# A hybrid decoder layer on one Trainium2 core: split input weights stored once and reloaded, and the convolutions given other stretches of the program

## The chip, the cores and the metric

The kernel runs on one core of a Trainium2 chip. The metric is the device time of one execution in microseconds (us). A run of a kernel is one such time; a profile is one further execution, recorded instruction by instruction. The chip's engines go by the profile's names: PE is TensorE (matmuls; PEld its weight loads), DVE is VectorE, ACT is ScalarE, POOL is GpSimd, SP is SyncE, which here only issues transfers (DMAs), in the order of its queue.

## What is computed

One layer of a decoder on 2048 tokens (16 more "meta" tokens are put in front and dropped at the end), with 1024 features, all in float32. Cut to what matters here:

```python
s = layer_norm(concat(meta, x))                       # (2064, 1024)
u = s @ w_in                                          # 1024 -> 2576 columns
c_val, c_gate, q, k, v, r, g_down = split(u)          # 512, 512, 256, 256, 512, 512, 16
h = c_val * sigmoid(c_gate)
conv_out = silu(layer_norm(causal_depthwise_conv(h, width=31) + conv_b))
o = gated_linear_attention(q, k, v, log_sigmoid(g_down @ gate_up + gate_bias) / 16)
gla_out = rms_norm(o) * silu(r)
s = layer_norm(alpha * s + concat(conv_out, gla_out) @ w_out)
s = layer_norm(alpha * s + relu(s @ w_ff1) ** 2 @ w_ff2)
```

## The kernel before, in words

**Number format.** Float32 products are made from two parts. A tile is split into `hi`, the value cast to the rounded type fp32r by ScalarE, and `lo`, the remainder that VectorE subtracts (`split`, L189 to L191). A product is then three matmuls: hi x hi, hi x lo, lo x hi. Weights and activations alike are split on the core, each time that they are loaded.

**Stages.** The 2048 tokens are four groups of 512 (`s` = 0 to 3). For each group the input projection `win_units(s)` runs as a pass over all of `w_in`: in groups 1 to 3 the gate and value columns of the convolution branch (`gate_val`), the attention values V, the forget gate, R, then K and Q; group 0 takes V first, while its tokens are still being normalised, and carries the meta tokens along. A pass needs 40 slabs of weights (256 KB each, 128 partitions x 512 numbers). Then come the output projections of groups 0 and 1 (`wout_units`), feed-forward 1 and 2 of the first half (`ff1s_units`, `ff2_units`, a fast matrix scheme with seven products), the output projections of groups 2 and 3, and the feed-forward of the second half. In feed-forward 1 the first ten weight groups have two of their seven products done ahead, so that five remain (`order`, L1000).

**Slabs.** `load_w` (L193) makes one slab: a raw tile from a pool of four (`rawp`), a DMA on SP's queue (L197 for two row blocks of 256 columns, L200 for one of 512), a slab tile from a ring of ten (`wp`, 512 KB each with both parts) and the split (cast at L190, subtraction at L191). Every pass fetches and splits every slab again: four passes x 40. A channel unit (gate, value, K, Q; `ch_units`, `ch_matmul`, L472 to L474) uses four slabs for 24 matmuls of 512 columns; a token unit (V, R; `tok_units`, L394 to L396) uses one slab for 12.

**Convolution.** Each group's convolution `conv(s)` (L717) takes four channel tiles. It reloads one (`hin`, two buffers, L724), starts the sum on ScalarE (L727) and adds 30 taps with one VectorE instruction each (L730, out `cacc`), so 120 for a group. Then it transposes, normalises (L737 to L758) and stores its half of the mixer's input (`mixd`, L760), which the output projection loads and splits (`mix_load`, tile `mraw`).

**Order.** `Program` holds the matmul work as a list of units with costs, and side streams: generators that are stepped in proportion to the costs that have passed between a start and an end unit (`prog.side`, L1337 and on). The convolutions are side streams, and each of their steps carries a lowered priority (`later`, L764). A scheduler then arranges the instructions of each engine by its own estimate of when they can run; each engine runs them in that order. So a convolution's stretch is a guide, and the built order says where its steps stand. `bounds[s]` is the first unit of pass `s`, `m_wout` that of the output projection, `m_f20` that of feed-forward 2 of the first half, `W[s].gv_end` the end of a pass's gate and value units. `prog.defer(n, fn)` runs `fn` n units later.

**Feed-forward 1.** Each weight group loads two raw tiles (`w1r`, L971, in the ring of ten), forms operand sums from them on VectorE (L978; `s` is the first difference), splits them into operands (`wop`), multiplies (L1007 to L1009), combines the products of the group before on VectorE (L1041; `p`, `u`, `a`, `h`, `s` are its tiles) and stores results through SP's queue (`hor`, L1014). A w1r load stands behind such stores in SP's queue.

Of the kernel before, what the change touches and what calls it, by code (L numbers as in the profile page):

```python
# [10 lines left out]
F32 = mybir.dt.float32  # L11
F32R = mybir.dt.float32r
# [5 lines left out]
P = 128  # L18
# [6 lines left out]
KD = D // P  # L25
# [23 lines left out]
CONV_LATE = 100  # L49
# [96 lines left out]
def hymba_kernel(ctx: ExitStack, tc: tile.TileContext, x, meta, ln_in_g, ln_in_b, w_in, small, gate_up,  # L146
                 w_out, ln1_g, ln1_b, w1, w2, ln2_g, ln2_b, out):
    nc = tc.nc
# [4 lines left out]
    wp = ctx.enter_context(tc.tile_pool(name="wp", bufs=RING))  # L153
# [4 lines left out]
    dp = ctx.enter_context(tc.tile_pool(name="dp", bufs=1, space=bass.MemoryType.DRAM))  # L158
# [19 lines left out]
    prog = Program(RING)  # L178

    def mm_tile():  # L180
        return mmp.tile([P, 512], F32, tag="mm", name="mm")
# [7 lines left out]
    def split(hi, lo, src, eng=None):  # L189
        nc.scalar.copy(hi, src)  # L190
        (eng or nc.vector).tensor_tensor(out=lo, in0=src, in1=hi.bitcast(F32), op=ALU.subtract)  # L191

    def load_w(src, nk, eng=None):  # L193
        def fn():
            raw = rawp.tile([P, 512], F32, tag="raw", name="raw")
            if nk == 2:
                nc.sync.dma_start(out=raw.rearrange("p (k c) -> p k c", k=2),  # L197
                                  in_=src.rearrange("(k p) c -> p k c", p=P))
            else:
                nc.sync.dma_start(out=raw, in_=src)  # L200
            sl = wp.tile([P, 2, 512], F32R, tag="w", name="wsl")
            split(sl[:, 0, :], sl[:, 1, :], raw, eng)
            return sl
        return prog.load(fn)

    def loads_ch(w, c0):
        return [load_w(w[k2 * 256:(k2 + 1) * 256, c0:c0 + 256], 2) for k2 in range(KD // 2)]

    def loads_tok(w, c0):
        return [load_w(w[k * P:(k + 1) * P, c0:c0 + 512], 1) for k in range(KD)]  # L210

    def rstd_of(out_, var, n):
        p = out_.shape[0]
# [81 lines left out]
    def load_x(s, tt):  # L295
        t = xin[s, tt] = pa.tile([P, D], F32, tag="xin", name="xin", bufs=2)
        nc.sync.dma_start(out=t, in_=x[s * SUB + tt * P:s * SUB + (tt + 1) * P, :])

    def prep_tile(s, tt):
        if s or tt == 0:  # L300
            load_x(s, tt)
        t = xin[s, tt]
        if s == 0 and tt == 0:
            nc.sync.dma_start(out=A.g, in_=ln_in_g.partition_broadcast(P))
            nc.sync.dma_start(out=A.b, in_=ln_in_b.partition_broadcast(P))
            load_x(0, 1)
        yield
        st = stats_bn(t) if s == 0 and tt < NBN else stats_act(t, None, pa, "sg")
        if s == 0 and tt == 0:
            prog.pre(RING)  # L310
            consts()
        yield
        yield from ln_apply(t, st, A.g, A.b)
        nc.sync.dma_start(out=s0d[s][tt], in_=t)
        yield from transpose_split(t, xt[s], tt)
# [129 lines left out]
    W = {}  # L445

    def win_units(s):
        w = W[s] = NS()
# [41 lines left out]

        def first_units(c0, evac):
            nonlocal xtm
            ls = [load_w(w_in[k * P:(k + 1) * P, c0:c0 + 512], 1, nc.gpsimd if k % 2 else None) for k in range(KD)]

            def unit(tt):
                for _ in prep_tile(0, tt):
                    pass
                if 0 < tt + 1 < TT - 1:
                    load_x(0, tt + 2)
                ps = mm_tile()  # L500
                for k in range(KD):
                    tok_mm(ps, prog.slot[ls[k]], k, tt)
                evac(tt, ps)

            def unit_meta():
                nonlocal xtm
                xtm = prep_meta()
                um = meta_matmul(lambda k: [prog.slot[ls[k]][:, hl, :] for hl in range(2)], 512)
                pv = gl_tile()
                nc.tensor.matmul(pv, i2, um, start=True, stop=True)  # L510
                w.vm = pa.tile([P, 512], F32, tag="og", name="vm")
                nc.scalar.copy(w.vm, pv)

            for tt in range(TT):
                prog.add(lambda tt=tt: unit(tt), ls, 5.2)
            prog.add(unit_meta, ls, 3.5)
# [246 lines left out]
    CONV_N = CT * CW + TT * 3  # L763

    def later(gen, offset):
        while True:
            with tc.high_priority(offset=-offset):
                try:
                    next(gen)
                except StopIteration:  # L770
                    return
            yield
# [534 lines left out]
    m_wout = prog.mark()  # L1307
# [8 lines left out]
    m_f20 = ff_units(0, late[0])  # L1316
    m_w2 = prog.mark()
# [15 lines left out]
    bounds = m_win + [m_wout]  # L1333
# [2 lines left out]
    for s in range(NSUB - 1):  # L1336
        prog.side(gla(s), GLA_N, bounds[s + 1], W[s + 1].gd)  # L1337
    prog.side(gla(NSUB - 1), GLA_N, m_wout - 1, m_wout)
    prog.side(later(conv(0), CONV_LATE), CONV_N, W[0].gv_end, bounds[1] + 16)
    prog.side(later(conv(1), CONV_LATE), CONV_N, W[1].gv_end, bounds[3])  # L1340
    prog.side(later(conv(2), 100), CONV_N, W[3].gv_end, m_f20)
    prog.side(later(conv(3), 100), CONV_N, m_f20, m_w2 - 4)
    prog.side(ln2_sub(0), 3 * TT, m_w2, m_w3)
    prog.side(ln2_sub(1), 3 * TT, m_w3, m_ff1)
    prog.emit()
# [30 lines left out]
```

## Time and profile before

| what | us |
|---|---|
| median of the runs shown (2109.33, 2111.32, 3585.48) | 2111.32 |
| the profiled execution's own time | 2108.08 |
| its span, first to last instruction | 2106.4 |
| TensorE busy in it | 2021.8 |
| VectorE busy | 1650.7 |
| ScalarE busy | 1005.3 |

A matmul is counted as busy until its modelled end, though the next one starts before, so the busy time of TensorE tells only where it stood quite still. Read beside it the count of matmuls in a stretch. Lines are those of the kernel before; a line can be a helper's (L190 and L191 are all splits), so the tile's name says which use it is. "<-" behind a wait names what ended it.

### The profile page before, as it was taken

The page shows a single profiled execution, that of the slowest core. Times are in us where ns is not written, and L with a number is a line of the kernel's source. Part 1 is how long each engine was busy: PE and PEld are TensorE (multiplying, and loading weights), DVE is VectorE, ACT ScalarE, POOL GpSimd, SP SyncE. Part 2 cuts the span into 40 slices and gives each one's busy share as a digit, 9 for nine tenths or more (in the row PEclk, how much of TensorE's full clock was granted, in tenths as well). Part 3 has the DMA queues.
Part 4 walks back from the last instruction along what each step waited for, and adds up shares of the span by engine and source line. Part 5 has one row for each costly group of instructions (what it writes and reads, how often), then busy time and mean ns, then how long its engine had stood idle before and what let it go on. Part 6 is the DMA issues. An engine that isn't in the chain of part 4 may idle for free. (4 is left out here: it accounts for less than half of the span.)

```text
span 2106.4 us, 26294 instructions
## 1 busy us (share of the span) xinstructions
PE 2021.8 (96%) x9144; PEld 1647.0 (78%) x9144; DVE 1650.7 (78%) x2658; ACT 1005.3 (48%) x1720; POOL 93.7 (4%) x104
## 2 busy tenths in 40 slices
PE   6999999999989999999999999999999999999996
PEld 4878878878777777778778788777777787788885
DVE  6599989989988677776699999579877765644875
ACT  3564474554543454455653434455644554433342
POOL 3000100100000000000000000011000000000001
PEclk9999999999999999999999999999999999999998
DMA  5533434534346556654899877277666548965761
GB/s 185 172 111 107 147 110 122 162 90 130 107 125 205 191 185 209 205 180 144 284 331 390 311 251 273 70 242 252 198 204 206 183 140 291 320 203 197 251 221 70
DMA packets 245285, 409.39 MB, mean 194 GB/s; under 512 B 21424, under 2 KB 115856, under 8 KB 245152
## 3 DMA queue, kind: packets, MB, share of 16 engines
q1 hardware_dynamic: 226144, 368.91, 53.2%
q10 hardware_dynamic: 19008, 38.81, 4.9%
q8 instruction: 72, 1.18, 0.2%
q14 instruction: 61, 0.50, 0.1%
HBM read 297.29 MB, written 110.35 MB: 194 GB/s over the span
## 5 line engine op out<-in xcount | busy, mean ns | idle before, releaser
L730 DVE SCALAR_TENSOR_TENSOR cacc<-hin,sm,cacc 128x512 f32<-128x512 f32 x480 | 344.6, 745 | 2.0
L1218 PE MATMUL mm<-op 128*128 128x512 f32 x544 | 213.3, 392 | 7.0 <-ACT op L190 7.0
L190 ACT CAST wsl<-raw 128x512 fp32r<-128x512 f32 x224 | 136.6, 620 | 168.0 <-PE mm L396 40.5
L1219 PE MATMUL mm<-op 128*128 128x512 f32 x544 | 212.8, 391 | 0.0
L1220 PE MATMUL mm<-op 128*128 128x512 f32 x544 | 211.3, 390 | 0.0
L190 ACT CAST op<-wr 128x1024 fp32r<-128x1024 f32 x92 | 92.5, 1051 | 223.0 <-PE mm L1220 163.2
L191 DVE TENSOR_TENSOR op<-wr,op 128x1024 fp32r<-128x1024 f32 x92 | 108.9, 1219 | 80.2 <-ACT op L190 80.1
L191 DVE TENSOR_TENSOR wsl<-raw,wsl 128x512 fp32r<-128x512 f32 x220 | 149.4, 690 | 24.9 <-ACT wsl L190 24.6
L1007 PE MATMUL gl<-x,wop 128*128 128x512 f32 x384 | 152.1, 397 | 7.8 <-DVE a L1041 3.0
L394 PE MATMUL mm<-xt,wsl 128*128 128x512 f32 x384 | 153.8, 400 | 0.0
L395 PE MATMUL mm<-xt,wsl 128*128 128x512 f32 x384 | 152.4, 397 | 0.0
L396 PE MATMUL mm<-xt,wsl 128*128 128x512 f32 x384 | 152.2, 397 | 0.0
L1008 PE MATMUL gl<-x,wop 128*128 128x512 f32 x384 | 150.7, 392 | 0.0
L1009 PE MATMUL gl<-x,wop 128*128 128x512 f32 x384 | 150.2, 392 | 0.0
L1218 PEld LDWEIGHTS mm<-op 128*128 128x128 f32 x544 | 102.7, 189 | 29.6 <-ACT op L190 7.9
L190 ACT CAST wop<-w1r 128x512 fp32r<-128x512 f32 x152 | 91.0, 616 | 67.0 <-DVE w1r L978 38.0
L1219 PEld LDWEIGHTS mm<-op 128*128 128x128 f32 x544 | 102.7, 189 | 21.3
L1220 PEld LDWEIGHTS mm<-op 128*128 128x128 f32 x544 | 102.4, 188 | 21.4 <-DVE op L191 0.2
L191 DVE TENSOR_TENSOR op<-lr,op 128x1024 fp32r<-128x1024 f32 (+1 forms) x92 | 104.8, 1172 | 16.7 <-ACT op L190 16.7
L191 DVE TENSOR_TENSOR wop<-w1r,wop 128x512 fp32r<-128x512 f32 x152 | 103.7, 687 | 17.5 <-ACT wop L190 16.8
L1007 PE MATMUL mm<-xt,wop 128*128 128x512 f32 x256 | 100.9, 397 | 5.2 <-ACT a L1047 5.2
L1007 PE MATMUL mm<-x,wop 128*128 128x512 f32 x256 | 100.4, 396 | 1.5 <-ACT x L190 0.8
(282 smaller groups left out, 4811.5 us busy)
## 6 DMA issues: line engine op xcount, KB each, us to landing
wr<-in_w_dram SPq DMA_DIRECT2D x120, 512.0 KB, 6.1
lr<-hor SPq DMA_DIRECT2D x108, 512.0 KB, 6.0
raw<-in_w_in_dram SPq DMA_DIRECT2D x160, 256.0 KB, 2.9
w1r<-in_w_dram SPq DMA_DIRECT2D x64, 512.0 KB, 5.2
wr<-td SPq DMA_DIRECT2D x40, 512.0 KB, 5.4
raw<-in_w_out_dram SPq DMA_DIRECT2D x64, 256.0 KB, 4.1
hor<-s SPq DMA_DIRECT2D x64, 256.0 KB, 3.0
raw<-in_w_dram SPq DMA_DIRECT2D x40, 256.0 KB, 4.0
```

The costliest lines, as they stand in the source:

```text
L190: nc.scalar.copy(hi, src)
L191: (eng or nc.vector).tensor_tensor(out=lo, in0=src, in1=hi.bitcast(F32), op=ALU.subtract)
L394: nc.tensor.matmul(ps, wh, mov(k, 0), start=(k == 0), stop=False)
L395: nc.tensor.matmul(ps, wh, mov(k, 1), start=False, stop=False)
L396: nc.tensor.matmul(ps, wl, mov(k, 0), start=False, stop=(k == KD - 1))
L730: nc.vector.scalar_tensor_tensor(out=acc, in0=h[:, j:j + SUB], scalar=wc(j), in1=acc, op0=ALU.mult, op1=ALU.add)
L1007: nc.tensor.matmul(ps, wh, X[i][:, k, 0, :], start=start and k == 0, stop=False, skip_group_check=not start)
L1008: nc.tensor.matmul(ps, wh, X[i][:, k, 1, :], start=False, stop=False, skip_group_check=not start)
L1009: nc.tensor.matmul(ps, wl, X[i][:, k, 0, :], start=False, stop=(k == 3), skip_group_check=not start)
L1218: nc.tensor.matmul(ps, lh, rt[n][:, p, 0, :], start=(q == 0 and p == 0), stop=False)
L1219: nc.tensor.matmul(ps, lh, rt[n][:, p, 1, :], start=False, stop=False)
L1220: nc.tensor.matmul(ps, ll, rt[n][:, p, 0, :], start=False, **ends)
```

## The change

In the first group's pass each split slab is also stored to a DRAM tile (`wkd`, 512 KB, one unit after its load). In the other three passes the slab is loaded from there with one DMA straight into the ring, without a raw tile and without a split. Apart from that, the four convolutions have other start and end units.

```diff
--- before.py
+++ after.py
@@ -190,8 +190,14 @@
         nc.scalar.copy(hi, src)
         (eng or nc.vector).tensor_tensor(out=lo, in0=src, in1=hi.bitcast(F32), op=ALU.subtract)
 
-    def load_w(src, nk, eng=None):
+    wkd = {}
+
+    def load_w(src, nk, eng=None, kept=None):
         def fn():
+            if kept is not None and kept in wkd:
+                sl = wp.tile([P, 2, 512], F32R, tag="w", name="wsl")
+                nc.sync.dma_start(out=sl.bitcast(F32), in_=wkd[kept].bitcast(F32))
+                return sl
             raw = rawp.tile([P, 512], F32, tag="raw", name="raw")
             if nk == 2:
                 nc.sync.dma_start(out=raw.rearrange("p (k c) -> p k c", k=2),
@@ -200,14 +206,18 @@
                 nc.sync.dma_start(out=raw, in_=src)
             sl = wp.tile([P, 2, 512], F32R, tag="w", name="wsl")
             split(sl[:, 0, :], sl[:, 1, :], raw, eng)
+            if kept is not None:
+                d = wkd[kept] = dp.tile([P, 2, 512], F32R, name=f"wkd{kept}")
+                prog.defer(1, lambda: nc.sync.dma_start(out=d.bitcast(F32), in_=sl.bitcast(F32)))
             return sl
         return prog.load(fn)
 
     def loads_ch(w, c0):
-        return [load_w(w[k2 * 256:(k2 + 1) * 256, c0:c0 + 256], 2) for k2 in range(KD // 2)]
+        return [load_w(w[k2 * 256:(k2 + 1) * 256, c0:c0 + 256], 2, kept=c0 + k2 if w is w_in else None)
+                for k2 in range(KD // 2)]
 
     def loads_tok(w, c0):
-        return [load_w(w[k * P:(k + 1) * P, c0:c0 + 512], 1) for k in range(KD)]
+        return [load_w(w[k * P:(k + 1) * P, c0:c0 + 512], 1, kept=c0 + k if w is w_in else None) for k in range(KD)]
 
     def rstd_of(out_, var, n):
         p = out_.shape[0]
@@ -490,7 +500,8 @@
 
         def first_units(c0, evac):
             nonlocal xtm
-            ls = [load_w(w_in[k * P:(k + 1) * P, c0:c0 + 512], 1, nc.gpsimd if k % 2 else None) for k in range(KD)]
+            ls = [load_w(w_in[k * P:(k + 1) * P, c0:c0 + 512], 1, nc.gpsimd if k % 2 else None, kept=c0 + k)
+                  for k in range(KD)]
 
             def unit(tt):
                 for _ in prep_tile(0, tt):
@@ -1336,10 +1347,10 @@
     for s in range(NSUB - 1):
         prog.side(gla(s), GLA_N, bounds[s + 1], W[s + 1].gd)
     prog.side(gla(NSUB - 1), GLA_N, m_wout - 1, m_wout)
-    prog.side(later(conv(0), CONV_LATE), CONV_N, W[0].gv_end, bounds[1] + 16)
-    prog.side(later(conv(1), CONV_LATE), CONV_N, W[1].gv_end, bounds[3])
-    prog.side(later(conv(2), 100), CONV_N, W[3].gv_end, m_f20)
-    prog.side(later(conv(3), 100), CONV_N, m_f20, m_w2 - 4)
+    prog.side(later(conv(0), CONV_LATE), CONV_N, W[0].gv_end, bounds[1] + 14)
+    prog.side(later(conv(1), CONV_LATE), CONV_N, bounds[1] + 14, bounds[2] + 21)
+    prog.side(later(conv(2), CONV_LATE), CONV_N, bounds[2] + 21, m_wout)
+    prog.side(later(conv(3), CONV_LATE), CONV_N, m_wout, m_f20 + 60)
     prog.side(ln2_sub(0), 3 * TT, m_w2, m_w3)
     prog.side(ln2_sub(1), 3 * TT, m_w3, m_ff1)
     prog.emit()
```

**In the built order, VectorE in feed-forward 1, first half, one of the groups with five products.** `s`, `p`, `u`, `a`, `h` are as above; lines of the changed kernel stand 11 higher there (L989 is L978, L1052 is L1041, L741 is L730). Before:

```order
L978 TENSOR_TENSOR s_7506<-w1r 128x512
L1041 TENSOR_TENSOR p_7479<-p_7479,gl 128x512
L1041 TENSOR_TENSOR p_7479<-p_7479,a_7334 128x512
L978 TENSOR_TENSOR w1r<-w1r 128x4x128 x2
L1041 TENSOR_TENSOR u_7458<-u_7458,mm 128x512
L978 TENSOR_TENSOR w1r<-w1r 128x4x128
L191 TENSOR_TENSOR wop<-w1r,wop 128x4x128 x2
L1041 TENSOR_TENSOR s_7528<-h_7336,u_7458 128x512
```

and now:

```order
L989 TENSOR_TENSOR s_7456<-w1r 128x512
L741 SCALAR_TENSOR_TENSOR cacc<-hin,sm,cacc 128x512 x2
L1052 TENSOR_TENSOR p_7429<-p_7429,gl 128x512
L741 SCALAR_TENSOR_TENSOR cacc<-hin,sm,cacc 128x512
L1052 TENSOR_TENSOR p_7429<-p_7429,a_7285 128x512
L989 TENSOR_TENSOR w1r<-w1r 128x4x128
L1052 TENSOR_TENSOR u_7409<-u_7409,mm 128x512
L989 TENSOR_TENSOR w1r<-w1r 128x4x128
L741 SCALAR_TENSOR_TENSOR cacc<-hin,sm,cacc 128x512
L989 TENSOR_TENSOR w1r<-w1r 128x4x128
L191 TENSOR_TENSOR wop<-w1r,wop 128x4x128
```

Four steps of the last convolution (L741) stand between the difference and the first operand split; a fifth stands ahead of the difference.

**SP's queue in the first pass, from the value product of the first channel tile.** `hd` is the store of the convolution's input, `s0d` that of the normalised tokens, `raw` a load of weights. Before:

```order
L297 DMA xin<-in_x_dram 128x1024 x2
L197 DMA raw<-in_w_in_dram 128x2x256 x8
L314 DMA s0d_0_96<-xin 128x1024
L609 DMA hd_0_108<-h 128x512
L613 DMA hd_0_112<-h 128x30
L297 DMA xin<-in_x_dram 128x1024
L197 DMA raw<-in_w_in_dram 128x2x256 x2
```

and now, where `wkd` is the store of a split slab:

```order
L211 DMA wkd_682<-wsl 128x1024
L211 DMA wkd_688<-wsl 128x1024
L620 DMA hd_0_108<-h 128x512
L624 DMA hd_0_112<-h 128x30
L324 DMA s0d_0_96<-xin 128x1024
L203 DMA raw<-in_w_in_dram 128x2x256 x4
L307 DMA xin<-in_x_dram 128x1024
L211 DMA wkd_837<-wsl 128x1024
L211 DMA wkd_843<-wsl 128x1024
```

Stores of slabs now stand ahead of the stores of `hd`, and the next raw loads behind both.

**SP's queue in the second pass, at its first value products.** Before:

```order
L724 DMA hin<-hd_2_110 128x542
L197 DMA raw<-in_w_in_dram 128x2x256 x8
L724 DMA hin<-hd_3_111 128x542
L609 DMA hd_0_112<-h 128x512
L613 DMA hd_0_116<-h 128x30
L197 DMA raw<-in_w_in_dram 128x2x256 x2
L200 DMA raw<-in_w_in_dram 128x512
L711 DMA mixd_1_233<-go 512x1x128
```

and now (L199 loads a split slab, L735 the convolution's input):

```order
L199 DMA wsl<-wkd_682 128x1024
L199 DMA wsl<-wkd_688 128x1024
L735 DMA hin<-hd_2_110 128x542
L620 DMA hd_0_112<-h 128x512
L624 DMA hd_0_116<-h 128x30
L199 DMA wsl<-wkd_837 128x1024
L199 DMA wsl<-wkd_843 128x1024
L199 DMA wsl<-wkd_849 128x1024
L199 DMA wsl<-wkd_855 128x1024
```

The slab loads stand in the queue where raw loads stood, one for one, with the convolution's loads among them.

## Rows read from the trace of the kernel before

**Rows 1.** The page, busy time of one engine (share of the span) and instructions.

```profile
PE 2021.8 (96%) x9144; PEld 1647.0 (78%) x9144; DVE 1650.7 (78%) x2658; ACT 1005.3 (48%) x1720; POOL 93.7 (4%) x104
```

**Rows 2.** Windows: stretch; length; busy PE, PEld, DVE, ACT, POOL (instructions); clock; DMA share; GB/s.

```profile
0.00:75.00 75.00, 57.09 (x246) 44.20 (x247) 45.00 (x83) 32.96 (x58) 17.23 (x26) 0.98 0.57 184
...
595.00:695.00 100.00, 96.25 (x473) 78.23 (x472) 84.29 (x169) 40.01 (x92) 8.60 (x8) 1.00 0.53 175
...
750.00:901.00 151.00, 146.46 (x633) 115.77 (x632) 118.48 (x189) 74.80 (x134) 0.00 (x0) 1.00 0.61 199
...
1055.00:1170.00 115.00, 113.92 (x503) 94.37 (x504) 108.03 (x116) 49.27 (x57) 0.00 (x0) 1.00 0.97 365
...
1800.00:1850.00 50.00, 50.00 (x222) 41.40 (x221) 28.28 (x25) 19.82 (x22) 0.00 (x0) 1.00 0.90 314
```

**Rows 3.** Waits of TensorE, 150 to 300 and 450 to 600 us: total, times, longest.

```profile
PE tp L751 <- ACT cn L748: 2.0, 2, 1.2
...
PE tp L578 <- DVE e L572: 3.7, 1, 3.7
...
PE tp L751 <- ACT cn L748: 2.3, 3, 1.1
...
PE mm L410 <- ACT gd L403: 1.9, 1, 1.9
```

**Rows 4.** Windows, the stretch behind the longest of those waits.

```profile
583.40:590.20 6.80, 6.01 (x16) 4.88 (x17) 6.01 (x11) 3.29 (x7) 0.00 (x0) 0.50 0.49 155
```

**Rows 5.** The page, costliest groups: busy, mean ns; idle before.

```profile
L190 ACT CAST wsl<-raw 128x512 fp32r<-128x512 f32 x224 | 136.6, 620 | 168.0 <-PE mm L396 40.5
...
L191 DVE TENSOR_TENSOR wsl<-raw,wsl 128x512 fp32r<-128x512 f32 x220 | 149.4, 690 | 24.9 <-ACT wsl L190 24.6
```

**Rows 6.** Groups by line, VectorE's convolution steps, 0 to 600 and 1050 to 1345 us.

```profile
L730 DVE SCALAR_TENSOR_TENSOR cacc<-hin,sm,cacc 128x512 f32<-128x512 f32 x329 | 236.2, 744 | 0.8
...
L730 DVE SCALAR_TENSOR_TENSOR cacc<-hin,sm,cacc 128x512 f32<-128x512 f32 x120 | 85.5, 746 | 0.8
```

**Rows 7.** Timeline of VectorE and SP in feed-forward 1: start, us, instruction, wait before it.

```profile
800.21 0.69 DVE L978 TENSOR_TENSOR s<-w1r 128x512 f32<-128x512 f32 x1 [2.55 <-DMA w1r<-in_w_dram]
...
808.01 0.68 DVE L1041 TENSOR_TENSOR u<-u,p 128x512 f32<-128x512 f32 x1
...
808.72 0.32 SPq L1014 DMA_DIRECT2D hor<-u  x1
...
809.15 0.38 SPq L971 DMA_DIRECT2D w1r<-in_w_dram  x1
...
815.13 0.69 DVE L978 TENSOR_TENSOR s<-w1r 128x512 f32<-128x512 f32 x1 [2.82 <-DMA w1r<-in_w_dram]
...
815.74 0.68 DVE L1041 TENSOR_TENSOR p<-p,gl 128x512 f32<-128x512 f32 x1
```

**Rows 8.** Waits of VectorE, 750 to 901 us.

```profile
DVE s L978 <- DMA w1r<-in_w_dram: 18.6, 10, 2.8
...
DVE w1r L978 <- DMA w1r<-in_w_dram: 8.9, 9, 2.6
```

**Rows 9.** The page, DMA issues: KB each, median us to landing.

```profile
wr<-in_w_dram SPq DMA_DIRECT2D x120, 512.0 KB, 6.1
...
raw<-in_w_in_dram SPq DMA_DIRECT2D x160, 256.0 KB, 2.9
...
xin<-in_x_dram SPq DMA_DIRECT2D x16, 512.0 KB, 3.7
```

**Rows 10.** Waits of TensorE, 1050 to 1350 and 1350 to 1450 us.

```profile
PE mm L1218 <- ACT ac L1233: 2.0, 1, 2.0
...
PE mm L1218 <- ACT op L190: 1.9, 1, 1.9
...
PE tp L751 <- ACT cn L748: 1.3, 2, 0.7
```

**Rows 11.** Waits of SP's queue, 150 to 600 us.

```profile
SPq L724 <- DVE cacc L730: 37.3, 8, 10.9
```

## The prediction, on record before the changed kernel ran

> **What bounds the kernel now.** I read the page's busy times first, then the windows stage by stage, then the waits of each engine inside a stage, and last the timeline of the stage where a chain of waits shows. TensorE is busy for 2021.8 of 2106.4 us [rows 1], so the whole kernel is nearly a stream of matmuls, and only its gaps can be won or lost. How full a stage is I take from matmul counts. In an untroubled window of 50 us there are 222 matmuls of 512 columns [rows 2], that is 0.2252 us each. The first half's stage "feed-forward 1" (FF1), 750 to 901 us, shows 633 matmuls in 151 us: 633 x 0.2252 = 142.6 us at most, as a few of them are shorter, so over 8 us of it are gaps, though its busy column leaves 4.5 [rows 2].
>
> The Trainium skill ("Trainium Kernel Development and Optimization", Performance Expectations) says that matmul busy time is a bad measure of distance to the limit because matmuls are pipelined, and that weight-load busy time is a good one. The trace agrees: weight loads are 41.40 of 50 us in the full window and 115.77 of 151 us here, so 151 x (1 - 0.767 / 0.828) = 11 us of gaps. By the busy column TensorE would be within 3% of its limit here and the loop described below would hardly bind; by the page it binds already, and what lengthens it is paid in full.
>
> In the four input-projection passes (0 to 600 us) the waits that TensorE names after 150 us are short: on the transposes of the convolution's norm, once on the key transposes (3.7 us) and once on the gate (1.9) [rows 3]. None of these waits names a weight slab, although every slab is cast on ScalarE and subtracted on VectorE before use. After the 3.7 us gap the granted clock is 0.50, its lower level, for 6.8 us [rows 4]: 16 matmuls in 6.8 us instead of about 30. So 3.2 us more belong to that gap.
>
> **The change, part by part.**
>
> *Splits removed.* Three passes x 40 slabs = 120 slabs need neither the cast (620 ns) nor the subtraction (690 ns) [rows 5]: 120 x 0.620 = 74 us of ScalarE and 120 x 0.690 = 83 us of VectorE. Neither engine ends the chain in these passes; TensorE waits on them only in the rows named. The waits after 150 us are 2.0 + 3.7 + 2.3 + 1.9 [rows 3] and three smaller ones of 2.2 together, 12.1 us, and 3.2 us of clock: at most 15 us to win, at least nothing. I take 8: the key gap and its clock loss (6.9), since the slab splits and the splits of the mixer's input that stand between its instructions on VectorE and ScalarE leave or move ahead, and 1 of the rest. What is late next there is the gate chain, which in the last pass now has 12 convolution steps queued ahead of its subtraction.
>
> *Convolution moved.* Each convolution is 120 steps of 745 ns on VectorE. The order of VectorE shows where they stand. Before, 321 of 480 stand ahead of the last pass's final key product; the trace has 329 by 600 us, and all 120 of the last convolution in feed-forward 2 (FF2) [rows 6]; FF1 has none. Now 360 stand ahead of that key product (39 more, 29 us, against 83 removed), 56 between there and the first main load of FF1 (39 before), and 64 in FF1's main groups, where none stood. FF2 loses all of its 120, 89 us.
>
> *FF1, the term that decides.* Its first ten groups of five products run in a loop over VectorE, the SP queue and a transfer. The rows show one turn: a sum `u` at 808.01, its store and the w1r load behind it in SP's queue at 808.72 and 809.15, the operand difference waiting 2.82 us for that load and starting at 815.13; the same instruction of the turn before started at 800.21 [rows 7]. So a turn is 14.9 us, while 60 matmuls need 60 x 0.2252 = 13.5. Over 750 to 901 us VectorE waits 18.6 us on the first w1r and 8.9 on the second [rows 8]: about 2.8 + 0.7 a turn. Into each turn the new order puts five convolution steps: one ahead of the difference (inside the 2.8 us wait: free), two right behind it and one between the two `p` sums, and one between the w1r sums. An instruction of 0.69 us is followed after 0.61 (815.13 to 815.74) [rows 7], so a step of 0.745 takes some 0.66 of the engine. The three in the middle add 2.0 us ahead of a w1r sum that waited 0.7, so 1.3 remain; the one between the sums adds 0.66. Both lie on the way from the landing of w1r to the `u` store that lets the next w1r go: 14.9 + 1.96 = 16.8 us a turn. Groups 2 to 9 carry this pattern: 8 x 1.96 = 15.7 us. Groups 0 and 1 also carry the norm of the second half and I leave them at nothing; from group 10 a turn has seven products, 84 x 0.2252 = 18.9 us of TensorE, which covers 16.8. Bounds: 0, if the 27.5 us of waits took all steps; 51 steps x 0.745 = 38 if none were hidden. A gain is excluded, as work is only added there. I take 15.
>
> The Trainium skill ("Perfetto Trace Analysis", Tensor Engine Instruction) notes that the queues of VectorE and ScalarE are strictly first in, first out. The trace agrees: the `p` sum behind the waiting difference starts only at 815.74 [rows 7]. If the queue could be passed, the term would be 0; this is the first rival's time.
>
> *Output projection, 595 to 695 us.* 56 - 39 = 17 more steps, 12.7 us, on a VectorE that was busy for 84.29 of 100 [rows 2]. Between 0 and 12.7; I take 3, since 15.7 us were idle but not where the steps stand.
>
> *Loads of split slabs.* 120 loads of 512 KB instead of 256 KB. The old ones landed in 2.9 us; a 512 KB load of 4 KB rows, as x's, in 3.7, the slowest kind in 6.1 [rows 9]. They go straight into the ring of ten slabs, so SP waits for a slab to come free, and the four raw buffers that ran ahead are gone. A gate or value unit is 24 matmuls, 5.4 us. Its slab is freed some 4 us before the second unit of its kind ends, then a value unit and half a gate unit pass before the slot's new slab is used: 4.1 + 5.4 + 2.7 = 12.2 us against 3.7 to 6.1. I take 0; 6 us are spare.
>
> *Stores in the first pass.* 40 stores of 512 KB, 21 MB, and each waits in SP's queue for its subtraction, with the raw loads of the next slabs behind it. In 0 to 75 us the core moved 184 GB/s [rows 2], 13.8 MB; with 22 stores 25.3 MB, or 338 GB/s, below the 365 that it sustains at 1055 to 1170 us [rows 2]. A group of raw loads now leaves after the splits of the group before: it loses its head start, at worst load, cast and subtraction, 2.9 + 0.62 + 0.69 = 4.2 us a group. The ring holds ten slabs, so most is hidden. Bounds 0 and 8 groups x 4.2 = 34; I take 2, near the hidden end, since ten slabs in hand last longer than 4.2 us.
>
> *FF2 and the second output projection.* FF2 at 1055 to 1170 us holds 503 matmuls, 113 us of 115 [rows 2]: nearly full with the convolution in it. Its waits are 2.0 and 1.9 us on ScalarE, and 1.3 us on the convolution's norm behind it [rows 10]. Gain 0 to 5; I take 3.
>
> **Sum.** The profiled execution took 2108.08 us. 2108.1 + 15 + 3 + 0 + 2 - 8 - 3 = 2117. The two closely agreeing runs are 2109.33 and 2111.32, some 2 above it: 2119 us, 0.4% over the median shown. A measurement of this kernel can tell about 2% (42 us) from no change, so this is "the same".
>
> **Rivals.**
> *The steps fit into the waits.* If the w1r landing moves with the new order, or takes less than the 6 us of rows 7, FF1 costs nothing: 2119 - 15 = 2104. For it: 27.5 us of waits stand against 51 x 0.66 = 34 us of steps, nearly enough. Against it: one step in five stands in the long wait. 0.25.
> *The first pass starves.* Raw loads behind stores behind splits: if the four gate and value groups each lose 4.2 us, 17 in place of 2: 2134. For it: 338 of 365 GB/s is near what the core sustains. Against it: the ring. 0.10.
> *The three later passes starve (the slower side).* SP's queue has waited up to 10.9 us at one load of the convolution's input for VectorE [rows 11]. A slab load behind that leaves 10.9 us late; with 6.1 to land, 17.0 against 12.2, TensorE loses 4.8 us. It decides from a block over 6.1 us at the moment a gate or value slab comes free; at 4 groups in 3 passes 12 x 4.8 = 58: 2177. Against it: only four of these loads fall in a pass, mostly in the token units, where a slab has ten units of 2.7 us. 0.05.
> *It doesn't do what it says.* If VectorE stays the late engine in the passes, the 8 us are not won: 2127; inside the range, and I give it no chance of its own.
> The forecast itself has 0.60, with 2108 to 2130 as its own range.
>
> **Numbers.** The range 2094 to 2140 reaches the first rival with some more of the 15 us of the passes won (2104 - 10), and the second with 6 over; it leaves out the third and the ends. Slower by over 2% (above 2153.5): 0.05 of the third rival and 0.01 of several terms at their ends, 0.06. Faster by over 2% (below 2069): all gains at their bounds give 2108 - 15 - 5 = 2088, so 0.02 for what I don't see. Within 2%: 0.92.
>
> **What would show it.** In the changed profile: no cast or subtraction of input slabs after the first pass; conv steps of 745 ns between w1r sums in FF1, with the difference instructions 16 to 17 us apart where they were 14.9, and fewer matmuls per us there; the 3.7 us key gap and its half-clock stretch gone; FF2 no longer than before by its matmul count. The forecast is wrong if the turn stays near 15 us, if TensorE's waits in 150 to 600 us name wsl, or if the first 150 us grow by over 10.

## The result, and the profile after

The changed kernel takes 2143.74 us (median of five runs, 2142.65 to 2147.34) against 2109.33: the ratio is 1.0175, 95% interval 1.0163 to 1.0187. One of the five runs of the kernel before took 3585.48 us, and the ratio leaves it out, so it is not quite the quotient of the two medians. That is 34 us slower, within the 2% called "the same", but outside the predicted range (2094 to 2140).

The page after, busy times, answers to [rows 1]; its DMA issues, KB each and median us to landing, to [rows 9]:

```profile
span 2141.9 us, 25907 instructions
...
PE 2035.9 (95%) x9144; PEld 1657.1 (77%) x9144; DVE 1580.3 (74%) x2538; ACT 943.1 (44%) x1608; POOL 92.8 (4%) x104
...
wsl<-wkd SPq DMA_DIRECT2D x120, 512.0 KB, 4.7
...
wkd<-wsl SPq DMA_DIRECT2D x40, 512.0 KB, 4.7
```

VectorE lost 120 instructions and 70 us of work, ScalarE 112 and 62 us; the span grew by 35.5. So less work on these two engines did not make the kernel faster.

Where the time went is read from matmuls that both kernels have. The view of one line's instructions gives their first and last start (the two times after "ns"). Before, L394 is a product of the channel units, with which a pass ends, L867 of the output projections (first and second half), L1218 of FF2. (The kernel's description has two ranges of lines the wrong way round: `ch_matmul` is L394 to L396, the token units are L472 to L474.)

```profile
L394 PE MATMUL mm<-xt,wsl x384: 387/389/628, 46.1 to 598.6; 128*128 128x512 f32 x192
...
L867 PE MATMUL mm<-wsl,xt x64: 387/389/585, 600.4 to 711.5; 128*128 128x512 f32 x64
...
L1218 PE MATMUL mm<-op x272: 389/389/499, 1041.3 to 1341.2; 128*128 128x512 f32 x136
L1218 PE MATMUL mm<-op,ox x96: 387/389/497, 1067.1 to 1355.3; 128*128 128x512 f32 x96
...
L867 PE MATMUL mm<-wsl,xt x64: 387/389/476, 1359.2 to 1454.5; 128*128 128x512 f32 x64
...
L1218 PE MATMUL mm<-op,ox x96: 389/389/389, 1807.5 to 2089.7; 128*128 128x512 f32 x96
```

and after (L404, L878, L1229):

```profile
L404 PE MATMUL mm<-xt,wsl x384: 387/389/628, 49.8 to 611.4; 128*128 128x512 f32 x192
...
L878 PE MATMUL mm<-wsl,xt x64: 387/389/482, 613.7 to 730.7; 128*128 128x512 f32 x64
...
L1229 PE MATMUL mm<-op x272: 387/389/792, 1067.1 to 1382.2; 128*128 128x512 f32 x136
L1229 PE MATMUL mm<-op,ox x96: 387/389/478, 1098.3 to 1393.1; 128*128 128x512 f32 x96
...
L878 PE MATMUL mm<-wsl,xt x64: 389/389/400, 1395.1 to 1487.6; 128*128 128x512 f32 x64
...
L1229 PE MATMUL mm<-op,ox x96: 388/389/390, 1843.0 to 2125.2; 128*128 128x512 f32 x96
```

The differences of these ends, stage by stage and from the unrounded times: four passes +12.7 us, output projection +6.5, FF1 up to FF2's first matmul +6.5, FF2 +12.0, second output projection -4.6, the rest +2.4; together 35.5, the whole growth of the span. The same table for the other kernels stands below.

**FF1.** The window that answers to [rows 2] (the same stretch, 19 us later), and one turn, which answers to [rows 7]:

```profile
769.00:920.00 151.00, 140.53 (x589) 109.47 (x588) 134.66 (x218) 67.25 (x123) 0.00 (x0) 0.98 0.57 186
```

```profile
839.79 0.69 DVE L989 TENSOR_TENSOR s<-w1r 128x512 f32<-128x512 f32 x1 [1.56 <-DMA w1r<-in_w_dram]
840.39 1.41 DVE L741 SCALAR_TENSOR_TENSOR cacc<-hin,sm,cacc 128x512 f32<-128x512 f32 x2
841.72 0.68 DVE L1052 TENSOR_TENSOR p<-p,gl 128x512 f32<-128x512 f32 x1
842.32 0.75 DVE L741 SCALAR_TENSOR_TENSOR cacc<-hin,sm,cacc 128x512 f32<-128x512 f32 x1
...
849.05 0.69 DVE L1052 TENSOR_TENSOR u<-u,p 128x512 f32<-128x512 f32 x1
849.77 0.32 SPq L1025 DMA_DIRECT2D hor<-u  x1
...
855.66 0.69 DVE L989 TENSOR_TENSOR s<-w1r 128x512 f32<-128x512 f32 x1 [1.65 <-DMA w1r<-in_w_dram]
```

There are 589 matmuls where there were 633, 44 x 0.2252 = 9.9 us fewer. The turn from difference to difference is 15.9 us (14.9 before). Over the eight turns from the third difference to the eleventh, the timeline gives 128.3 us, 115.9 before, so 16.0 and 14.5 a turn. The steps stand where the order had them: from difference to `u` sum it now takes 849.05 - 839.79 = 9.26 us (808.01 - 800.21 = 7.80 in [rows 7]), and the wait for w1r is shorter (1.6 us, 2.8 before).

**FF2.** TensorE's waits there (1060 to 1260 us; total, times, longest), and VectorE around the longer of the norm's:

```profile
PE tp L762 <- ACT cn L759: 7.0, 3, 4.2
PE mm L1229 <- ACT op L190: 6.6, 1, 6.6
```

```profile
1171.46 1.23 DVE L1179 TENSOR_TENSOR wr<-wr 128x1024 f32<-128x1024 f32 x1 [6.00 <-DMA wr<-td]
1172.60 0.69 DVE L770 TENSOR_TENSOR cy<-cy,csg 128x512 f32<-128x512 f32 x1
1173.20 0.69 DVE L750 BATCH_NORM_STATS2 cbn<-tp 128x6 f32<-128x512 f32 x1
```

The last convolution's norm now stands in the middle of FF2. Its statistics are queued on VectorE behind an operand sum that waits 6.00 us for a transfer; its transposes (L762) stand in TensorE's own queue, in front of matmuls that are ready.

**Passes.** TensorE's waits, 180 to 612 us, after; they answer to [rows 3]:

```profile
PE tp L762 <- ACT cn L759: 4.9, 4, 2.6
PE mm L420 <- ACT gd L413: 4.1, 1, 4.1
PE tp L719 <- DVE og L714: 3.4, 7, 0.8
PE tp L748 <- DVE cacc L741: 2.2, 2, 1.1
```

The 3.7 us key gap is gone, and none names wsl. The gate waits 4.1 us instead of 1.9, and the transposes of convolution and attention wait more often. The first pass ends 7.0 us later than before (181.1 us, 174.1 before); the second is 6.2 us longer, the third 10.0 longer, the last 10.4 shorter.

That the gap is gone does not show that the change removed it. The run e10 below leaves the passes as they were: up to 600 us its trace has the same instructions of TensorE, VectorE and ScalarE as that of before, in the same order. There the key gap is 0.9 us, in this line of TensorE's waits from 540 to 700 us:

```profile
PE tp L578 <- DVE e L572: 0.9, 1, 0.9
```

No half-clock stretch stands behind it, and the passes end 4.8 us earlier than in the profile of before. In e11 the gap is 2.1 us and they end 3.3 us earlier. So most of the 3.7 us belonged to that one execution.

**The clock.** Windows of five of the half-clock stretches after (the column before the DMA share is the granted clock), beside [rows 4]:

```profile
301.60:305.00 3.40, 2.78 (x11) 2.59 (x12) 2.98 (x7) 3.02 (x7) 0.99 (x1) 0.50 0.57 185
567.90:571.30 3.40, 3.39 (x8) 2.74 (x9) 3.22 (x6) 2.54 (x5) 0.00 (x0) 0.50 0.00 0
...
864.80:868.20 3.40, 3.40 (x10) 2.62 (x9) 3.40 (x6) 2.15 (x5) 0.00 (x0) 0.50 0.65 222
1083.30:1090.10 6.80, 5.16 (x12) 4.10 (x13) 5.89 (x9) 6.26 (x7) 0.55 (x1) 0.50 0.77 257
1178.80:1182.20 3.40, 3.26 (x10) 2.78 (x11) 2.63 (x3) 2.16 (x6) 0.00 (x0) 0.51 1.03 380
```

Between start-up and the final tail the trace has 54.4 us of such stretches, 20.4 before. At half rate the 34 more cost some 17 us, an estimate (a little less where TensorE also stood still): nearly half of the loss. The mean granted clock, too, is lower in all five runs of the changed kernel (0.983 to 0.985; 0.993 in the profile of before). They come behind the waits named above: the one at 301.6 behind a wait on the norm (the 2.6 us one), the one at 567.9 behind the gate's, the one at 864.8 behind a wait of 1.7 us in FF1, the one at 1083.3 behind the 6.6 us wait, the one at 1178.8 behind the norm's.

### The profile page after: what moved, and what is told of

Read it like the earlier page. It is cut to its first block, busy times and chain, and to the rows that moved or that the text cites. A ratio compares the mean times of both kernels' runs of the same rounds, so it can differ in the third digit from the quotient of the medians.

```text
span 2141.9 us, 25907 instructions
## 1 busy us (share of the span) xinstructions
PE 2035.9 (95%) x9144; PEld 1657.1 (77%) x9144; DVE 1580.3 (74%) x2538; ACT 943.1 (44%) x1608; POOL 92.8 (4%) x104
## 5 line engine op out<-in xcount | busy, mean ns | idle before, releaser
L741 DVE SCALAR_TENSOR_TENSOR cacc<-hin,sm,cacc 128x512 f32<-128x512 f32 x480 | 344.7, 747 | 4.9 <-ACT cacc L738 1.8
L1229 PE MATMUL mm<-op 128*128 128x512 f32 x544 | 214.9, 395 | 12.9 <-ACT op L190 12.9
L404 PE MATMUL mm<-xt,wsl 128*128 128x512 f32 x384 | 153.1, 399 | 0.0
L1229 PEld LDWEIGHTS mm<-op 128*128 128x128 f32 x544 | 103.7, 191 | 35.2 <-ACT op L190 13.7
L1018 PE MATMUL mm<-x,wop 128*128 128x512 f32 x256 | 103.3, 406 | 9.8 <-ACT wop L190 6.7
L190 ACT CAST op<-lr 128x1024 fp32r<-128x1024 f32 (+1 forms) x92 | 89.6, 1010 | 37.1 <-DMA lr<-hor 37.1
L1019 PE MATMUL mm<-x,wop 128*128 128x512 f32 x256 | 103.0, 402 | 0.1
```

What stands on the lines that cost most here:

```text
L404: nc.tensor.matmul(ps, wh, mov(k, 0), start=(k == 0), stop=False)
L741: nc.vector.scalar_tensor_tensor(out=acc, in0=h[:, j:j + SUB], scalar=wc(j), in1=acc, op0=ALU.mult, op1=ALU.add)
L1018: nc.tensor.matmul(ps, wh, X[i][:, k, 0, :], start=start and k == 0, stop=False, skip_group_check=not start)
L1019: nc.tensor.matmul(ps, wh, X[i][:, k, 1, :], start=False, stop=False, skip_group_check=not start)
L1229: nc.tensor.matmul(ps, lh, rt[n][:, p, 0, :], start=(q == 0 and p == 0), stop=False)
```

## The experiments

The starting theory: the loss comes from where the convolutions stand. The rival: it comes from the 160 transfers of 512 KB and their places in SP's queue. Each stage's growth in us against the profile of before, from the view shown above; "us" are medians of runs, each ratio against the kernel before on the same chip. A profile is one execution, so single entries under some 5 us say little: the passes differ by 4.8 us between before and e10, with the same instructions there in the same order, and the first pass by 4.4 between e1 and e6, with the same instructions too. The profiled run of e1 took 4.3 us less than the median of its runs, those of e4 and e6 took 5.1 and 4.4 more.

| run | us | ratio, 95% | passes | out 1 | FF1 | FF2 | out 2 | rest |
|---|---|---|---|---|---|---|---|---|
| changed kernel | 2143.7 | 1.0175 | +12.7 | +6.5 | +6.5 | +12.0 | -4.6 | +2.4 |
| e1 reload alone | 2112.9 | 1.0008-1.0036 | +1.3 | -0.3 | -2.7 | +0.6 | +1.0 | +0.5 |
| e2 spread alone | 2138.4 | 1.0124-1.0163 | +10.7 | +10.9 | +4.5 | +10.6 | -5.4 | -1.2 |
| e3 conv 3 lines back | 2139.9 | 1.0137-1.0168 | +9.3 | +6.6 | +9.0 | +3.5 | +0.7 | +2.3 |
| e4 stores on ScalarE | 2141.6 | 1.0134-1.0168 | +11.4 | +6.4 | +6.4 | +12.4 | -1.1 | +3.0 |
| e5 conv 2, 3 back | 2123.7 | 1.0041-1.0079 | +13.6 | +0.1 | -0.7 | -1.4 | +0.7 | +0.6 |
| e6 conv 0, 1 back | 2133.5 | 1.0064-1.0125 | +3.4 | +6.7 | +12.3 | +10.7 | -6.4 | +2.7 |
| e7 store in pass 2 | 2109.4 | 0.9982-1.0012 | +1.1 | 0.0 | -0.3 | -1.4 | +0.3 | +1.0 |
| e8 store in pass 3 | 2110.7 | 0.9976-1.0009 | -0.6 | -0.3 | -0.5 | +3.8 | +0.4 | +2.0 |
| e9 mixer loads later | 2109.4 | 0.9989-1.0011 | -4.8 | +2.8 | -0.2 | -0.5 | +2.0 | +0.3 |
| e10 steps behind | 2133.2 | 1.0098-1.0136 | -4.8 | +0.3 | +14.2 | +12.5 | -0.2 | +0.8 |
| e11 steps ahead | 2123.2 | 1.0047-1.0091 | -3.3 | +0.5 | +9.1 | +9.8 | +0.1 | +0.4 |
| e12 conv 0 new | 2115.4 | 1.0019-1.0054 | +5.1 | -0.3 | +0.3 | -1.7 | +0.6 | +3.6 |
| e13 conv 1 new | 2113.5 | 1.0001-1.0032 | +4.1 | +1.0 | -2.7 | +2.6 | +0.8 | +1.1 |
| e14 conv 2 new | 2128.2 | 1.0076-1.0113 | -0.6 | +8.2 | +10.0 | +1.0 | +2.0 | -1.4 |

**Reload and spread apart.** e1 is the changed kernel with this edit; e2 is the kernel before with the same edit turned round.

```diff
-    prog.side(later(conv(0), CONV_LATE), CONV_N, W[0].gv_end, bounds[1] + 14)
-    prog.side(later(conv(1), CONV_LATE), CONV_N, bounds[1] + 14, bounds[2] + 21)
-    prog.side(later(conv(2), CONV_LATE), CONV_N, bounds[2] + 21, m_wout)
-    prog.side(later(conv(3), CONV_LATE), CONV_N, m_wout, m_f20 + 60)
+    prog.side(later(conv(0), CONV_LATE), CONV_N, W[0].gv_end, bounds[1] + 16)
+    prog.side(later(conv(1), CONV_LATE), CONV_N, W[1].gv_end, bounds[3])
+    prog.side(later(conv(2), 100), CONV_N, W[3].gv_end, m_f20)
+    prog.side(later(conv(3), 100), CONV_N, m_f20, m_w2 - 4)
```

> The stored and reloaded slabs alone; the four convolutions keep the stretches of the kernel before. My theory: the reload itself gives back a little in passes 1 to 3 and costs some 5 to 7 us in the first pass, and the loss of the changed kernel comes from the convolutions: 2105 to 2117 us, the FF1 turn back at 14.9 us and no convolution norm inside FF2. Rival (the extra 512 KB transfers and their place in SP's queue are the main cost): 2130 us or more, with FF1 and FF2 as in the kernel before and the loss in the first 600 us.

> The new stretches of the convolutions alone; every pass loads and splits its slabs as before. My theory: most of the loss is here: 2125 to 2140 us, of which FF1 some 11, FF2 some 5 to 8 and the passes some 6, as VectorE now has both the splits and more convolution steps in them. Rival (transfers are the main cost): 2110 us, within 5 of the kernel before.

Both totals are as the theory had them: 2112.9 and 2138.4. The reload costs 3 to 5 us (2112.9 - 2109.4, the median of before beside it, and 2143.7 - 2138.4), the spread 29; the rival falls. The parts of e2 are not those expected: FF1 grew by 4.5 us and not by 11, and the output projection, which was not named, by 10.9.

**The stores' queue.**

```diff
-  prog.defer(1, lambda: nc.sync.dma_start(out=d.bitcast(F32), in_=sl.bitcast(F32)))
+  prog.defer(1, lambda: nc.scalar.dma_start(out=d.bitcast(F32), in_=sl.bitcast(F32)))
```

> The changed kernel with the 40 slab stores issued from ScalarE's queue, so that no raw load stands behind a store that waits for a subtraction. If the first pass's 7 us are lost by the order in SP's queue: 2136 to 2139 us, with end of the first pass 4 to 7 us earlier. If they are lost by the 21 MB of traffic or by the ring of slabs that the stores hold longer: 2142 to 2146, as changed.

2141.6 us, not told apart from 2143.7, and by the trace the first pass ended 4.9 us later still. This does not clear SP's order: in this trace TensorE waits 12.3 us for normalised tokens up to 43.2 us, where the changed kernel waits 4.1, so the stores in ScalarE's queue brought a loss of their own.

**The last convolution back.**

```diff
-    prog.side(later(conv(3), CONV_LATE), CONV_N, m_wout, m_f20 + 60)
+    prog.side(later(conv(3), 100), CONV_N, m_f20, m_w2 - 4)
```

> The changed kernel with only the last convolution put back into FF2; the other three stay as changed. My theory: the FF1 turn falls from 16.0 to about 14.9 us (11 us back), the norm no longer stands at the head of TensorE's queue in the middle of FF2 (5 to 7 back): 2120 to 2127 us. Rival (the three earlier convolutions and the transfers carry the loss, and FF1's longer turn is made up later): 2138 to 2144.

Measured 2139.9; FF1 stays long, so the expectation fell. The edit did not do what I took it for: the view of the steps' line shows all of them done by 969.1 us, as in the changed kernel (970.6), where the kernel before ends at 1301.5. First row e3, then before:

```profile
L741 DVE SCALAR_TENSOR_TENSOR cacc<-hin,sm,cacc x480: 718/745/754, 141.9 to 969.1; 128x512 f32<-128x512 f32 x160
```

```profile
L730 DVE SCALAR_TENSOR_TENSOR cacc<-hin,sm,cacc x480: 718/745/756, 98.7 to 1301.5; 128x512 f32<-128x512 f32 x160
```

The scheduler brings the steps forward as soon as they can run. Only the norm went back, to FF2's end (its first tile apart, at 1090 us): FF2 takes 8.5 us less, the second output projection 5.3 more. In the runs the difference is 3.9 us, the norm's net price in the middle of FF2, but the two intervals overlap (1.0137 to 1.0168 and 1.0163 to 1.0187), so it is not clear of the noise.

**Pairs of convolutions.** Of the edit of e1, e5 makes only the lines of convolutions 2 and 3 in the changed kernel, e6 only those of 0 and 1.

> The changed kernel with convolutions 2 and 3 put back as before; 0 and 1 stay in their new stretches. In the built order this leaves 360 convolution steps ahead of the feed-forward 1 loop and none in it, as in the kernel before. My theory: everything behind the passes comes back (output projection 6, FF1 13, FF2 7, second output projection -5): 2143.7 - 21 = 2120 to 2124 us, with FF1's turn at 14.9. Rival (convolutions 0 and 1 carry the loss): 2130 or more.

> The changed kernel with convolutions 0 and 1 put back as before; 2 and 3 stay in their new stretches, so 64 steps still stand in the FF1 loop. My theory: only a part of the 11 us of the passes comes back: 2133 to 2139 us, FF1 as in the changed kernel. Rival (0 and 1 carry the loss): 2125 or less.

Both totals as the theory had it, and the two parts add up: over the reload alone, 0 and 1 cost 2123.7 - 2112.9 = 10.8 us and lengthen the passes only; 2 and 3 cost 2133.5 - 2112.9 = 20.6 and lengthen what follows, up to the end of FF2. 2112.9 + 10.8 + 20.6 = 2144.3, and 2143.7 was measured. The ratios, each against runs of before on its own chip, put the parts at some 8 and 15 us, with intervals of up to 13 us, so the split is known to a few us only.

**One convolution at a time**, each of these is e1 with one new line; e14's, to show one:

```diff
-    prog.side(later(conv(2), 100), CONV_N, W[3].gv_end, m_f20)
+    prog.side(later(conv(2), CONV_LATE), CONV_N, bounds[2] + 21, m_wout)
```

> The reload with convolution 0 alone in its new stretch (it ends two units earlier). My theory: two units matter little, 2112 to 2116 us against 2112.9 of the reload alone. Rival (convolution 0's norm carries the passes' loss): 2118 or more.

> The reload with convolution 1 alone in its new stretch (start 14 units into the second pass rather than behind its gate and value units). My theory: this carries the passes' loss: 2119 to 2124 us. Rival: 2112 to 2116.

> The reload with convolution 2 alone in its new stretch; the last convolution's lines are those of the kernel before, though in the built order 66 of its steps stand in the feed-forward 1 loop. My theory (the last convolution waits for the four accumulators that convolution 2 holds until its norm): nearly the whole loss of moving both, 2126 to 2134 us, FF1 longer by 13 to 16 us. Rival (the last convolution's own lines matter): 2118 or less.

e12 came as expected; e13 missed: convolution 1 alone costs 0.6 us over the reload, convolution 0 alone 2.5, and only both together 10.8. So no single edit carries the passes' loss. The traces place it: from e1 to e5 the second pass grows from 144.4 to 148.2 us (e12 has that too), the third from 134.4 to 146.3 (135.0 in e12, 141.0 in e13), and the last shrinks from 142.9 to 137.7 (137.2 in e13). In the third pass TensorE has no wait in e1 and 6.5 us of them in e5. e14's total came as expected (FF1 grew by 10.0, 12.7 over e1, where 13 to 16 were expected): convolution 2 alone brings 15.3 of the 20.6 us, and the steps' last start is again early though the last convolution's lines are untouched:

```profile
L741 DVE SCALAR_TENSOR_TENSOR cacc<-hin,sm,cacc x480: 721/744/768, 141.9 to 971.3; 128x512 f32<-128x512 f32 x160
```

In the kernel before, the last convolution stayed out of FF1 because convolution 2, with the same four accumulators (`bufs=4` of `cacc`), kept them until its norm at FF1's end. e14 shows that convolution 2's line decides it; that it does so by the accumulators is read from the code. No run changed the number of accumulators, but all 16 traces fit: the last convolution's first instruction starts 1 to 8 us ahead of the last norm tile of convolution 2, wherever that stands (1050.1 and 1051.3 us before, 655.9 and 660.0 in the changed kernel).

**Extra steps in FF1 of the kernel before**, which has none there. e10 adds behind the difference, e11 ahead of it (`lo` is half of the operand made last in the group before; the lines that keep that operand in `prev` are left out):

```diff
                         tt_(r.s3, r11, r21, ALU.subtract)
+                        if half == 0 and g < NFR:
+                            junk = cv.tile([P, 512], F32, tag="cn", name="junk", bufs=2)
+                            for n in range(5):
+                                nc.vector.scalar_tensor_tensor(out=junk, in0=r.s3.rearrange('p a b -> p (a b)'), scalar=sm[:, 0:1], in1=r.s3.rearrange('p a b -> p (a b)'),
+                                                           op0=ALU.mult, op1=ALU.add)
```

```diff
+                        if half == 0 and 0 < g < NFR:
+                            lo = prev[0][:, :, 1, :].bitcast(F32)
+                            for n in range(5):
+                                nc.vector.scalar_tensor_tensor(out=r.s3, in0=lo, scalar=sm[:, 0:1], in1=lo,
+                                                               op0=ALU.mult, op1=ALU.add)
                         tt_(r.s3, r11, r21, ALU.subtract)
```

> The kernel before with five extra VectorE instructions of a convolution step's form in each of the first ten groups of feed-forward 1, first half; each reads the difference, so all stand between the landing of w1r and the store of u. Their output is not used. My theory (where a step stands decides): 5 x 0.66 less the 0.7 us wait on the second w1r = 2.6 us a turn, FF1 longer by 20 to 26 us: 2129 to 2136. Rival (VectorE's total work decides, as in the 64 steps of the changed kernel, 11 to 13 us): 2118 to 2123, and the same as the next run.

> The same five extra instructions a group, written so that all stand ahead of the difference, in the wait for w1r; in the built order the two p sums and one u sum of the group before stand ahead of it too, and the norm of the third convolution falls into this stretch. Their output is overwritten. My theory: 3.3 us of steps and 1.8 of sums fill a wait of 2.8, and the 1.8 are saved behind: some 0.5 us a turn, FF1 longer by 0 to 6 us: 2109 to 2116. Rival (total work decides): as the run with the steps behind the difference.

The totals were 2133.2 and 2123.2: behind is dearer, but neither theory is left whole. That e10's total fell into the expected range is luck: FF1 grew by 14.2 us, not by 20 to 26, and FF2, which was in neither theory, by 12.5. The windows of 790 to 900 us (TensorE's and VectorE's columns first and third) of before, e10 and e11:

```profile
790.00:900.00 110.00, 107.42 (x458) 84.88 (x457) 85.34 (x138) 53.03 (x95) 0.00 (x0) 1.00 0.63 204
```

```profile
790.00:900.00 110.00, 101.00 (x419) 78.56 (x418) 97.17 (x156) 49.29 (x85) 0.00 (x0) 0.98 0.56 188
```

```profile
790.00:900.00 110.00, 99.44 (x430) 78.78 (x429) 105.29 (x176) 56.99 (x104) 2.40 (x3) 0.98 0.62 202
```

Behind, 39 matmuls are lost; ahead, 28, not nearly none. There VectorE is busy for 105.29 of 110 us and no longer waits for w1r: the five steps and what moved in filled it. For e11 changed more than the added steps. Convolution 2's norm came forward to 783 to 868 us, and behind it 78 of the last convolution's 120 steps ran ahead of FF2's first matmul, 7 of them in this window, though no convolution's lines were touched. That agrees with the accumulators' part above, and makes e11 no clean test of the place of a step. The likely reading is that place matters while VectorE has waits left, and that its total binds soon after. FF2 lost 12.5 and 9.8 us too, with waits on its operand splits; why was not settled.

**Is there a better kernel?** e7 is e1 with the slabs stored in the second pass, e8 in the third (`at == 2`; `at` is the pass, the lines that set it are left out):

```diff
-            if kept is not None:
+            if kept is not None and at == 1:
```

e9 is the kernel before with one call moved:

```diff
-        if s == NSUB - 1:
-            prog.add(lambda: mix_load(0), cost=0.01)
         for u in ch_units(C_K, k_evac, km_evac if s == 0 else None):
             prog.add(*u)
+        if s == NSUB - 1:
+            prog.add(lambda: mix_load(0), cost=0.01)
```

> A candidate: convolutions as before, slabs split in the first two passes, stored in the second, loaded in the third and fourth. If the first pass lost its 4 us to the stores, because it is the pass in which the tokens arrive too, this loss goes and the 6.6 us of the key gap in the last pass are still won: 2102 to 2106 us. If stores cost the same in any pass: 2109 to 2113.

> The same with the slabs stored in the third pass and loaded in the fourth alone. The win of the reload without the convolutions lay in the last pass (6.6 us by the end of its key product): 2102 to 2106 us if that is so. If the win needs all three loaded passes: 2109 to 2112.

> The kernel before with one thing moved: the loads and splits of the first group's mixer input are issued between the key and the query units of the last pass, no longer ahead of the key units. No slab is reloaded and no convolution moved. In the trace of before the 3.7 us key gap stands behind such a split on VectorE, which itself waits 2.18 us for a cast that waits for this load. My theory: the reload's only win (6.6 us by the end of the last key product) was this queue order and has nothing to do with the slabs: here it comes without the reload, 2102 to 2105 us. Rival (the win came from the 240 splits that leave VectorE and ScalarE): 2108 to 2111, with the gap still there or moved to the first matmul of the output projection.

All three are equal to the kernel before within 0.25%: none beats it, and the gains expected of them did not come. In e7 the first pass is free of loss and TensorE names no wait on the keys, but the passes together still end 1.1 us later. In e9 the key gap shrinks from 3.7 to 1.2 us and the passes end 4.8 us earlier without any reload; but so they do in e10, whose passes are those of before, and the runs of e9 show nothing. So e9 does not show that the gap was the order of the mixer's splits, and no run shows a gain that a reload could win there.

## Why the prediction was wrong

The forecast added 9 us to the profiled execution; the span grew by 35.5. Its terms, against the changed profile:

- **FF1, +15: the mechanism was right, the size too high.** The turn was forecast at 16.8 us and took 16.0, but the one turn that I read before (14.9) was longer than the mean of 14.5; the loop lost 9.9 us by its matmul count. The way from difference to `u` grew by 9.26 - 7.80 = 1.46 of the forecast 1.96, and the way from `u` to the next difference got shorter (849.05 to 855.66 is 6.61, 808.01 to 815.13 was 7.12). I had taken that one as fixed.
- **The passes, -8: the step that failed.** With the stores they were to be 6 us shorter, and they grew by 12.7. Two things were wrong. First, I counted 39 more convolution steps against 83 us of subtractions removed and put the move at nothing. But the new stretches of convolutions 0 and 1 cost 10.8 us (e5 over e1), while VectorE is less busy than before (367.5 of the 432 us from 180 on, 396.3 before). A sum of busy time did not show that. The likely reason, not tried by itself, is the order in the queues: the norm's transposes stand in TensorE's queue, and the gate's subtraction stands in VectorE's behind the steps. The prediction named the gate chain as late next, and gave it no price; its wait grew by 2.2 us, and a half-clock stretch follows. Second, 6.9 of the 8 us were the key gap and its clock loss in one execution. In e10 the same instructions have a gap of 0.9 us, so most of it was not there to win, and with the old spread (e1) the passes behind the first take 421.7 us, against 424.5 before and 420.8 in e10: no gain of the reload is shown.
- **Stores in the first pass, +2: too small.** The first pass ends 7.0 us later in the changed kernel and 4.1 to 8.6 later in the seven other runs with these stores on SP's queue; without them it moves by 1.1 at most. The rival of 4.2 us a group, 17 in all, did not come. The wait that grew is not on weights but on tokens being normalised: 4.1 us at 37.0, 2.0 at that place before, with 10.2 us of half clock behind it where there were 3.4.
- **Loads of split slabs, 0:** held. No wait names wsl, and the runs leave 3 to 5 us for the reload with all its parts. The slower rival was wrong.
- **Output projection, +3:** +6.5. I priced 17 steps, and not convolution 2's norm, which moved there from FF1's end. That norm's leaving FF1 may give back part of it: FF1 up to FF2's first matmul grew by 6.5 where its loop lost 9.9.
- **FF2 and the second output projection, -3: failed too.** +12.0 - 4.6 = +7.4. I took 89 us of steps out of FF2 and forgot what ends them: the norm comes earlier, into the middle of a full stage. It costs some 4 us there net (e3, not clear of the noise). The 6.6 us wait at its start, with the half-clock stretch behind it, was in no term. ScalarE's cast there waits for a load of FF1's stored results. In all runs with convolution 2's new line (e2, e3, e6, e14) this wait is 5.7 to 8.5 us; in e1, e5, e12 and e13, where that norm stands just ahead of it, 1.0 at most (1.9 before). That the norm used to cover it is likely, but was not tried by itself.
- **The clock.** One half-clock stretch was priced, the one that goes. Those that new gaps bring were in no term: some 17 us, the estimate above, spread over the stages' figures.

The Trainium skill ("TensorE: Matmul & The Clock Gate", Terms) puts the penalty of such time at the share of the clock that is lost, here half. The trace agrees: 8 matmuls in the 3.40 us from 567.9, where 15 fit at 0.2252 us each. The Trainium skill's advice to avoid long idle gaps mid-kernel (same page, Why this matters for your kernels) is not enough here: in the 15 us ahead of the stretch from 864.8 us there is one wait, of 1.7 us.

What stays open: which of the waits in the second and third pass makes convolutions 0 and 1 cost 10.8 us together where they cost 2.5 and 0.6 apart, and what upsets FF2 in e10 and e11.

## What to carry to other kernels

When a side computation is moved, price what ends it, not only its steps: the transposes and norms that go through the engine that bounds the kernel, at the place where they will land. Ask which shared buffers held the next piece back, as a start unit in the code may not be what kept it there. Keep room in the sum for half-clock stretches behind new gaps on TensorE: a change that frees two side engines by 130 us can still lose 34. And before a gap of one profile is priced as a gain, look for it in a second execution of the same code.

## What the runs showed of the hardware that was not expected

A gap on TensorE can cost more than its length, and its length alone does not tell whether it will. In the changed kernel a wait of 1.7 us that ended at 863.4 was followed by 3.4 us of half clock, and one of 4.1 us (567.9) by as much; one of 3.3 us that ended at 1467.1 was followed by none, as this window shows:

```profile
1467.10:1475.00 7.90, 7.90 (x35) 6.54 (x36) 7.49 (x16) 4.93 (x9) 0.92 (x1) 1.00 0.70 202
```

The stretches, of 3.4 to 10.2 us there, add up: 20.4 us before, 27.2 in e7 and e9, 54.4 in the changed kernel, 64.7 in e4.
